# Four buffers for the split weights, tables that say how many are split ahead, and new orders of the units

## The chip, the core and the metric

The kernel runs on one core of one Trainium2 chip. Five engines work there side by side, each through its own list of instructions in order: TensorE (PE in the profile; PEld is its weight load), VectorE (DVE), ScalarE (ACT), GpSimd (POOL) and SyncE (SP), which here only issues DMAs. They wait for each other through semaphores. The metric is the device time of one execution in microseconds (us), the median of several runs; a profile is one execution with every instruction recorded.

## What is computed

Two transformer layers over 256 positions of width 2048, all in float32. Layer A: a norm, one projection to queries, keys, values and a forget gate, attention with 16 heads of 128, an output projection, a residual, then an MLP. Then keys and values for layer B are made once from the result, and layer B has its own queries, attention in chunks of 64, an output projection and an MLP. The MLP, on which this text turns, is

```python
def sq_relu_mlp(h, g, w1, w2):
    a = jax.nn.relu(rms_norm(h, g) @ w1)      # w1: 2048 x 8192
    return (a * a) @ w2                       # w2: 8192 x 2048
```

## The kernel before

**Three products per product.** A float32 weight is taken apart into two numbers that TensorE multiplies fast: `hi`, which ScalarE makes by copying the weight to the type fp32r, and `lo`, which VectorE makes as weight minus `hi`. The activations are held in the same way. `passes` then issues three rounds of matmuls: hi times hi (L592), hi times the activations' lo (L594), lo times hi (L596). The part of the weight that is split at a time is called a unit: 128 partitions by 1024 columns. It costs one ScalarE copy (L292), one VectorE subtraction (L293), and 12 matmuls of 512 columns when it is a plain unit.

**Seven products for eight.** In the MLPs and the query projection, a *pair* (two output panels `a` and `b`, both for both halves of the positions) does part of its depth by seven products of sums in place of eight products. The seven *forms* f0 to f6 are the weight block 11, then T3, T2, T1, 21, T4, 22: `FORMS = ("11", "T3", "T2", "T1", "21", "T4", "22")`. Each form has two units, each with only 6 matmuls. The sums of weight blocks are made on the way: T3 and T1 by a DMA that GpSimd issues and that adds as it writes (`add_on`, L324), T2 by VectorE (`make`, L331), T4 by VectorE (`add_on`, L322). The rest of the depth is 4 plain units for panel a (a4 to a7) and 4 for panel b (b4 to b7). The forms accumulate in four PSUM tiles, and three of these have to be combined on the way (the end of `form_products`): after f0 ScalarE writes `c`, after f1 it copies `P7`, after f2 VectorE makes `P7 - c` (L637) and after f3 `c - P7` (L639). f3 accumulates in the tile of `c`, and panel a's plain units in the tile that L637 writes, so both have to wait for L637. The names of the PSUM tiles alternate with the pair: `acc` in two of four, `s` and `po` in the others.

**The order.** A chunk of the MLP is four pairs: w10 and w11 (first weight matrix), w20 and w21 (second). Each layer has four chunks; layer A ends with the query pairs q0 and q1. `ORDER` holds a string per pair with the place of every unit: `f2` is both units of a form, `a` and `b` are this pair's next plain unit, `r` is a plain unit left over from the pair before (where none is left, it is passed over). `plan_mlp` turns it into one list, and the main loop takes it item by item: `fetch` (which splits units ahead), the matmuls, then `run_fill`, which issues the steps of finished panels that are due. When a panel's last unit is done, its results go off: `w1` panels are transposed by VectorE (L441) into a tile `z`, moved by 16 small DMAs into a tile `q` (L456, half of them issued by SP, half by GpSimd), then ScalarE applies relu (L954), squares it into `hi` (L959) and in float32 (L961), and VectorE takes the difference (L965). `HIDDEN`, `LONG`, `SHORT` and `QUERY` say after how many units each of these steps is issued. `BEHIND` says after which form the next sums of weights are issued. The order on TensorE, VectorE, ScalarE and SP is the written one; the instructions of GpSimd are placed by the scheduler.

**How far ahead.** `fetch` keeps three units split: the one about to be multiplied and two more (`AHEAD = 2`). `hi` and `lo` have three buffers each, so the fourth `hi` waits until TensorE has finished with the first. Copy and subtraction of a unit are issued together:

```python
def fetch(ahead=AHEAD, early=EARLY):
    while (units or raws) and len(ready) <= ahead:
        issue()                     # hi by ScalarE, lo by VectorE
```

The raw weights of forms f4, f6 and of the plain units come into three buffers of 128 x 2048 (`wraw`, two units each) by DMAs of 1 MB that SP issues (L279). `wsp = pool("wsp", 3)` in the listing is the pool of `hi` and `lo`.

Of the kernel before, what the change touches and what calls it, by code (L numbers as in the profile page):

```python
# [28 lines left out]
AHEAD = 2  # L29
EARLY = 4  # L30
HIDDEN = (
# [4 lines left out]
)  # L36
UA = UN // 512
LONG = (
# [4 lines left out]
)  # L43
SHORT = (
# [4 lines left out]
)  # L49
REL = 384  # L50
QUERY = (0, 1, 15, 10, 5, 17, 5)
AGAIN = (0, 1, 2, 3, 5, 5, 7, 7)
ATT = ((8, 14, 18, 18, 10), (8, 8, 12, 12, 9))
BIAS = (3, 6, 7)
ORDER = {
# [9 lines left out]
}  # L65
BEHIND = {
    (0, 0): [(2, 1, "add", "T1", 0), (0, 1, "make", 0)],
    (0, 1): [(0, 1, "make", 1)],
# [4 lines left out]
}  # L73
SUBS = {"1": (2, 2), "2": (2, 2), "q": (2, 2)}
OPENING = (
    (23, "bring", "12", 0),
    (19, "bring", "12", 1),
    (6, "add", "T3", 0),
    (9, "add", "T3", 1),
    (3, "bring", "11", 0),  # L80
    (4, "bring", "11", 1),
)
# [16 lines left out]
def trunk(ctx: ExitStack, tc: tile.TileContext, t):  # L99
# [8 lines left out]
    PSUM = bass.MemoryType.PSUM  # L108
    wsp = pool("wsp", 3)
    acts = pool("acts", 8)  # L110
# [37 lines left out]
    gqk = const.tile([P, 2], F32, name="gqk")  # L148
    flipper = const.tile([P, P], F32, name="flipper")
    V.tensor_copy(flipper, ident[:, ::-1])  # L150

# [21 lines left out]
    class Pair:  # L173

        def __init__(self, big, src, stage, n, subs):
            self.big, self.stage, self.n, self.subs = big, stage, n, subs
# [27 lines left out]
    def plan_mlp(layer, query, tail):  # L204
# [7 lines left out]
        for i, p in enumerate(pairs):  # L212
            own = [i for q in "ab" for u in p.plain for i in p.items(f"{q}{u}")]
            for j in ORDER["first" if not i else p.stage[0] + str(p.n) + ("+" if p.stage == ("w2", NCH - 1) else "")].split():
# [33 lines left out]
    n_out = 4 * KT // UA - 4  # L248
    units.extend(halves_of((w_in[i] for i in range(w_in.shape[0])), False))
    tail_a = Tail(stage_units(w_oa, 4))  # L250
# [30 lines left out]

    def issue():
        if not raws:
            load()
        item, raw, cuts, _ = raws.popleft()
        if not cuts:
            assert (FORMS[item.u], item.s) in item.pair.done
            raw, cuts = item.pair.t[FORMS[item.u]][:, half(item.s)], [slice(0, UN)]
        hi = wsp.tile([P, UN], F32R, name="hi")
        lo = wsp.tile([P, UN], F32R, name="lo")  # L290
        for c in cuts:
            S.activation(hi[:, c], raw[:, c], AF.Copy)  # L292
            V.tensor_tensor(lo[:, c], raw[:, c], hi[:, c].bitcast(F32), op=ALU.subtract)  # L293
# [41 lines left out]
    def behind(p, i, s):  # L335
        for k in range(s, 2 if s == p.subs - 1 else s + 1):
            for d, own, f, *a in BEHIND.get((i, k), ()):
# [199 lines left out]
    class RowStats:  # L537
# [39 lines left out]
        def flip(self):  # L577
            pm = ps_o.tile([P, 512], F32, name="pt", tag="po")
            TE.matmul(pm[:, :NB], flipper, self.ms, start=True, stop=True)
            f = RowStats(self.name + "f")  # L580
# [348 lines left out]
    rooms.open()  # L929
    for g in range(NG):  # L930
        zq, lq = turned("z")
# [17 lines left out]
    def mlp(plan, x, Sx, st, last, query=None):  # L949
# [49 lines left out]
        for it in plan:  # L999
            p, hl = it.pair, fetch()  # L1000
            assert it.u < 4 or it.kind == "f" or it.u * 2 < len(p.x or range(99)), (p.stage, p.n, it.u, len(p.x))
# [9 lines left out]
            if it.kind != "f" or it.s == p.subs - 1:  # L1011
                run_fill()
                q = {"f4": 0, "f5": 0, "f6": 1}.get(f"f{it.u}") if it.kind == "f" else it.kind
                if q is not None:
                    p.left[q] -= 1
                    if not p.left[q]:
                        for b in range(NB):
                            p.evac[q](b, p.ps[q][b])

    st1, x1, S1 = RowStats("m"), [], []  # L1020
    stage(o, [next_x(n, None, st1, 1, x1, fs=S1, then=st1.inverse if n == NG - 1 else None) for n in range(NG)], tail=tail_a, plan=plan_a)
    st2, xb, kept = RowStats("b"), [], []
    xkv, Sq, qs = [], [], []

    def query(g):
        box = {}

        def f(b, ps):
            if b == 0:
                z, lq = turned(), landing(2 + g % 2)  # L1030
                box["lq"], box["f"] = lq, head_norm(lambda: st2, z, lq, apart=(*QUERY[:2], None, None)[g])
            box["f"](b, ps)
            if b == NB - 1:
                add_fill([[]] * QUERY[2 + g] + [[lambda: qs.append(scale_q(box["lq"], 1, g))]])
                if g == 1:
# [5 lines left out]
    mlp(plan_a, x1, S1, st1, lambda n, r2: next_x(n, r2, st2, 3, xb, kept, Sq, st2.both if n == NG - 1 else None), (xb, Sq, query))  # L1041
    st2f = st2.flipped

    def rel_bias(g, box):
# [9 lines left out]

    o = [None] * H
    rooms.open()
    for g in range(NG):
# [85 lines left out]
```

## Time and profile before

| | |
|---|---|
| three runs | 2113.25, 2117.59, 2120.19 us; median 2117.59 |
| the profiled execution | 2115.48 us; span of its instructions 2113.7 us |
| mean granted clock of TensorE in it | 0.998 |
| busy: PE, PEld, DVE, ACT, POOL | 2074.7, 1695.1, 1736.8, 1301.9, 354.1 us |
| DMA | 538.89 MB, mean 255 GB/s |
| MLP of layer A, queries, MLP of layer B | about 370 to 1060, 1060 to 1150 and 1425 to 2110 us of the span |

In rows of the time line, the columns are the start and the length in us, engine, source line, operation, tile written and tiles read, and how many equal instructions follow each other; in brackets is the idle time of the engine before it and what ended it. The length of one matmul there is that of its whole way through the array. The next one enters long before, so distances from start to start tell the rate. In rows of waits come the total in us, the number and the longest. In rows of windows come, for each engine, the busy us and the count of instructions, then TensorE's granted clock, the busy share of the DMA engines and GB/s.

### The profile page before, as it was taken

What the parts mean: (1) busy time and instruction counts of PE and PEld (TensorE: products, weight loads), DVE (VectorE), ACT (ScalarE), POOL (GpSimd) and SP (SyncE); (2) the same over time, 40 slices, a digit from 0 to 9 for tenths busy, and PEclk for the clock granted to TensorE, in tenths of its full rate; (3) what the DMA queues carried; (4) which work ended last, traced back from release to release, by engine and by line L of the source; (5) the groups of instructions that cost most, each with busy time, mean ns of one, the idle gap of its engine ahead of it and who ended that gap; (6) DMA issues with size and microseconds to landing.
All of it is one profiled execution on the core that took longest, in us unless ns stands there. A gap on an engine that the chain in (4) does not pass through costs nothing.

```text
span 2113.7 us, 27078 instructions
## 1 busy us (share of the span) xinstructions
PE 2074.7 (98%) x9114; PEld 1695.1 (80%) x9114; DVE 1736.8 (82%) x2003; ACT 1301.9 (62%) x1567; POOL 354.1 (17%) x552
## 2 busy tenths in 40 slices
PE   9999999999999999999999999999999999999999
PEld 7888888787887887887777888887878878878877
DVE  6777776998889889878989577768988998898897
ACT  6544445676567567557767445456765765675674
POOL 1101002221031022022224000022200310220220
PEclk9999999999999999999999999999999999999999
DMA  8777788889888888898786777888897898888884
GB/s 302 241 257 222 240 253 266 251 257 283 273 256 245 277 267 244 262 278 268 239 241 218 256 235 241 239 265 251 268 278 256 259 259 279 268 250 256 280 262 157
DMA packets 160636, 538.89 MB, mean 255 GB/s; under 512 B 42849, under 2 KB 68081, under 8 KB 125681
## 3 DMA queue, kind: packets, MB, share of 16 engines
q1 hardware_dynamic: 129136, 453.78, 61.3%
q0 software_dynamic: 31360, 83.39, 20.8%
q8 instruction: 71, 1.16, 0.2%
q14 instruction: 69, 0.56, 0.1%
HBM read 497.20 MB, written 15.75 MB: 243 GB/s over the span
## 4 chain that ended last, share of the span: by engine, by line
PE 83%; DMA 6%; DVE 6%; issue 3%; ACT 2%; SPq 0%; POOL 0%; ACTq 0%; DVEq 0%; POOLq 0%
PE acc L592 18%; PE acc L594 18%; PE acc L596 18%; PE po L592 5%; PE po L596 5%; PE po L594 5%; PE s L596 4%; PE s L592 4%; PE s L594 4%; DVE lo L293 3%; DMA raw<-in_s2a 2%; DMA q<-z 2%; ACT hi L292 2%; DVE wT L322 1%; DMA raw<-in_s2b 1%
## 5 line engine op out<-in xcount | busy, mean ns | idle before, releaser
L293 DVE TENSOR_TENSOR lo<-raw,hi 128x1024 fp32r<-128x1024 f32 (+1 forms) x634 | 759.5, 1214 | 221.2 <-ACT hi L292 208.9
L292 ACT ACTIVATE hi<-raw 128x1024 fp32r<-128x1024 f32 (+1 forms) x634 | 660.4, 1054 | 386.7 <-PE acc L594 224.5
L592 PE MATMUL acc<-hi,act 128*128 128x512 f32 x1644 | 459.0, 394 | 9.9 <-DVE acc L637 4.4
L596 PE MATMUL acc<-lo,act 128*128 128x512 f32 x1644 | 449.1, 390 | 0.3 <-DVE lo L293 0.3
L594 PE MATMUL acc<-hi,act 128*128 128x512 f32 x1644 | 449.1, 390 | 0.0
L592 PEld LDWEIGHTS acc<-hi,act 128*128 128x128 f32 x1644 | 306.1, 188 | 79.5 <-DVE acc L637 7.9
L596 PEld LDWEIGHTS acc<-lo,act 128*128 128x128 f32 x1644 | 307.5, 188 | 66.8 <-DVE lo L293 2.4
L594 PEld LDWEIGHTS acc<-hi,act 128*128 128x128 f32 x1644 | 308.5, 188 | 65.5 <-DVE act L387 0.5
L292 ACT ACTIVATE hi<-w 128x1024 fp32r<-128x1024 f32 x204 | 215.1, 1056 | 100.6 <-PE acc L594 39.6
L293 DVE TENSOR_TENSOR lo<-w,hi 128x1024 fp32r<-128x1024 f32 x204 | 244.5, 1216 | 27.9 <-ACT hi L292 27.2
L456 POOL DMA_DIRECT2D q<-z x336 | 174.1, 608 | 464.1 <-DVE z L441 253.8
L292 ACT ACTIVATE hi<-wT 128x1024 fp32r<-128x1024 f32 x136 | 142.4, 1057 | 65.7 <-PE acc L594 27.0
L293 DVE TENSOR_TENSOR lo<-wT,hi 128x1024 fp32r<-128x1024 f32 x136 | 162.7, 1218 | 21.9 <-ACT hi L292 21.8
L596 PE MATMUL s<-lo,act 128*128 128x512 f32 x476 | 137.7, 394 | 2.6 <-DVE lo L293 2.4
L592 PE MATMUL s<-hi,act 128*128 128x512 f32 x476 | 136.4, 391 | 0.8 <-ACT hi L292 0.8
L594 PE MATMUL s<-hi,act 128*128 128x512 f32 x476 | 135.5, 389 | 0.0
L596 PEld LDWEIGHTS s<-lo,act 128*128 128x128 f32 x476 | 87.9, 188 | 27.0 <-DVE lo L293 9.7
L592 PEld LDWEIGHTS s<-hi,act 128*128 128x128 f32 x476 | 89.4, 188 | 20.6 <-ACT hi L292 2.0
L594 PEld LDWEIGHTS s<-hi,act 128*128 128x128 f32 x476 | 89.5, 188 | 18.8
L691 POOL TENSOR_TENSOR rn<-vv,mhalf 128x4 f32<-128x4 f32 x32 | 44.3, 1398 | 336.4 <-DVE vv L690 336.3
L331 DVE TENSOR_TENSOR wT<-w,w 128x1024 f32<-128x1024 f32 x68 | 82.7, 1217 | 0.0
L322 DVE TENSOR_TENSOR wT<-wT,raw 128x1024 f32<-128x1024 f32 x68 | 82.7, 1216 | 0.0
(183 smaller groups left out, 2282.1 us busy)
## 6 DMA issues: line engine op xcount, KB each, us to landing
raw<-in_w_in SPq DMA_DIRECT2D x94, 512.0 KB, 5.5
raw<-in_s1a SPq DMA_DIRECT2D x32, 1024.0 KB, 6.4
raw<-in_s2a SPq DMA_DIRECT2D x32, 1024.0 KB, 6.9
raw<-in_w_kv SPq DMA_DIRECT2D x64, 512.0 KB, 5.5
raw<-in_s1b SPq DMA_DIRECT2D x32, 1024.0 KB, 7.0
raw<-in_s2b SPq DMA_DIRECT2D x32, 1024.0 KB, 6.7
raw<-in_w_oa SPq DMA_DIRECT2D x32, 512.0 KB, 6.3
w<-in_f1a SPq DMA_DIRECT2D x16, 1024.0 KB, 7.0
```

Of the source, the lines that this page charges most:

```text
L292: S.activation(hi[:, c], raw[:, c], AF.Copy)
L293: V.tensor_tensor(lo[:, c], raw[:, c], hi[:, c].bitcast(F32), op=ALU.subtract)
L322: V.tensor_tensor(d, d, p.t["21", s], op=ALU.add)
L331: V.tensor_tensor(p.t["T2"][:, half(s)], p.t["T3"][:, half(s)], p.t["11"][:, half(s)], op=ALU.add)
L456: (SY, G)[j % 2].dma_start(d[32 * j : 32 * j + 32, i], z[32 * i : 32 * i + 32, j * n : (j + 1) * n])
L592: TE.matmul(ps, xh, cut(hi, j), start=first, stop=False, **kw)
L594: TE.matmul(ps, xl, cut(hi, j), start=False, stop=False, **kw)
L596: TE.matmul(ps, xh, cut(lo, j), start=False, stop=last, **kw)
L691: G.tensor_tensor(rn, vv, mhalf, op=ALU.pow)
```

## The change

No arithmetic is added or removed: per engine the two programs issue the same operations, save that a copy of a mirrored identity (`flipper`) moves from the start of the kernel to the place of its only use.

- `hi` and `lo` get four buffers in place of three. Room for this comes from `flipper`, which now has a passing tile, and from the scratch space of GpSimd's DMAs, 2048 bytes a partition in place of 8192.
- `issue` is cut in two: `high` (ScalarE's copy) and `low` (VectorE's subtraction). `fetch` takes two numbers. `LOOK` says, by pair and form, how many units are wholly split ahead (2 before, now 1 to 3), and `MORE` how many more get their `hi` alone (0 to 2); at most four are open.
- `ORDER`, `HIDDEN`, `LONG`, `SHORT`, `QUERY` and the opening are dealt out anew, and `BEHIND` now has a table for each kind of pair.
- The scaled queries are kept by number, with checks of their order. `MINI` (off) builds the first MLP alone.

```diff
-    (1, 3, 3, 3, 6, 8, 8, 9, 11, 11),
+    (2, 3, 3, 5, 8, 8, 9, 10, 11, 12),
...
+LOOK = {
+    "w10": (2, 1, 2, 2, 3, 1, 2, 2),
...
+MORE = {
+    "w10": (1, 2, 0, 0, 0, 0, 0, 0),
...
-    "w11": "f0 r f1 r f2 f4 a r f3 r a a f5 a f6 b b",
-    "w20": "r f0 r r f1 f2 f4 f3 f5 a r r a r b f6 b",
-    "w21": "f0 f1 f2 r f3 f4 r a f5 r r f6 r b a r",
+    "w11": "f0 f1 r f2 r r f4 a f3 r a a r r f5 a f6 b b",
+    "w20": "r f0 r f1 f2 f4 r f3 f5 a r a f6 b r r",
+    "w21": "f0 f1 f2 r r f3 r f4 r r r r a f6 f5 r a b r",
...
-    wsp = pool("wsp", 3)
+    wsp = pool("wsp", AHEAD + 2)
...
-    def issue():
+    highs = deque()
+
+    def high():
         if not raws:
             load()
         item, raw, cuts, _ = raws.popleft()
...
         hi = wsp.tile([P, UN], F32R, name="hi")
+        for c in cuts:
+            S.activation(hi[:, c], raw[:, c], AF.Copy)
+        highs.append((item, raw, cuts, hi))
+
+    def low():
+        if not highs:
+            high()
+        item, raw, cuts, hi = highs.popleft()
         lo = wsp.tile([P, UN], F32R, name="lo")
         for c in cuts:
-            S.activation(hi[:, c], raw[:, c], AF.Copy)
             V.tensor_tensor(lo[:, c], raw[:, c], hi[:, c].bitcast(F32), op=ALU.subtract)
...
-    def fetch(ahead=AHEAD, early=EARLY):
-        while (units or raws) and len(ready) <= ahead:
-            issue()
+    def fetch(ahead=AHEAD, early=EARLY, more=0):
+        while (units or raws or highs) and len(ready) <= ahead:
+            low()
+        while (units or raws) and len(ready) + len(highs) <= ahead + more and can_high():
+            high()
...
-            p, hl = it.pair, fetch()
+            p = it.pair
+            if isinstance(p, Pair):
+                n = it.u if it.kind == "f" else 7
+                hl = fetch(LOOK[p.key][n], more=MORE[p.key][n])
+            else:
+                hl = fetch()
...
-    nc = bacc.Bacc("TRN2", target_bir_lowering=False, num_devices=1, dynamic_dma_scratch_size=8192)
+    nc = bacc.Bacc("TRN2", target_bir_lowering=False, num_devices=1, dynamic_dma_scratch_size=2048)
```

Three places show what the tables do. In all of them the names are those of the second chunk of layer A (the numbers are the program's own). `wT2` is the tile that holds T2 and later T4, `raw` is a block of raw weights.

VectorE, before, at form f4 of pair w11 (`raw_5002` is its block, `po_4718` and `po_4719` are panel b of w10, whose last unit b7 stands between f1 and f2 on TensorE; L322 makes T4):

```order
L441 STREAM_TRANSPOSE z_5172<-po_4718 128x4x4x32
L441 STREAM_TRANSPOSE z_5172<-po_4719 128x4x4x32
L293 TENSOR_TENSOR lo_5177<-raw_5002,hi_5176 128x1024
L322 TENSOR_TENSOR wT2_5040<-wT2_5040,raw_5002 128x1024
L293 TENSOR_TENSOR lo_5190<-raw_5002,hi_5189 128x1024
L322 TENSOR_TENSOR wT2_5040<-wT2_5040,raw_5002 128x1024
L637 TENSOR_TENSOR acc_5083<-p7_5153,acc_5084 128x512
L293 TENSOR_TENSOR lo_5209<-raw_5080,hi_5208 128x1024
```

The same engine and place in the change, where `raw_4978` is b7 of w10 (now between f2 and f4 on TensorE), `raw_4990` the block of f4, and L673 the former L637:

```order
L319 TENSOR_TENSOR lo_5151<-raw_4978,hi_5149 128x1024
L319 TENSOR_TENSOR lo_5164<-raw_4990,hi_5154 128x1024
L348 TENSOR_TENSOR wT2_5034<-wT2_5034,raw_4990 128x1024
L673 TENSOR_TENSOR acc_5076<-p7_5119,acc_5077 128x512
L319 TENSOR_TENSOR lo_5176<-raw_4990,hi_5167 128x1024
L348 TENSOR_TENSOR wT2_5034<-wT2_5034,raw_4990 128x1024
L475 STREAM_TRANSPOSE z_5195<-po_4719 128x4x4x32
L475 STREAM_TRANSPOSE z_5195<-po_4720 128x4x4x32
L319 TENSOR_TENSOR lo_5201<-raw_5090,hi_5199 128x1024
```

The combination after f2 moved from behind both units of f4 to between them, and the transposes from the front to the end.

ScalarE, before, in pair w20 (`raw_5403` holds a4 and a5, `raw_5557` b4 and b5, `raw_5637` f6; L954 is the relu of panel b of w11, which reads the `q` that the small DMAs write):

```order
L292 ACTIVATE hi_5633<-raw_5403 128x1024
L292 ACTIVATE hi_5645<-raw_5403 128x1024
L954 ACTIVATE q_5524<-q_5524 128x1024
L292 ACTIVATE hi_5661<-raw_5557 128x1024
L292 ACTIVATE hi_5681<-raw_5637 128x1024
```

The same in the change (`raw_5540` is f6, `raw_5616` b4 and b5, `w11_5660` f0 of the next pair; the relu is now L990):

```order
L310 ACTIVATE hi_5614<-raw_5403 128x1024
L310 ACTIVATE hi_5638<-raw_5403 128x1024
L310 ACTIVATE hi_5656<-raw_5540 128x1024
L310 ACTIVATE hi_5677<-raw_5540 128x1024
L310 ACTIVATE hi_5694<-raw_5616 128x1024
L310 ACTIVATE hi_5698<-w11_5660 128x1024
L310 ACTIVATE hi_5712<-w11_5660 128x1024
L990 ACTIVATE q_5525<-q_5525 128x1024
```

The relu moved behind five copies, among them that for b4.

VectorE, before, in pair w21, from the second T4 to the first unit of f6 (`raw_5686` is f4's block, `raw_5667` a7 of w20, `raw_5813` a4, `raw_5853` b6 and b7 of w20, `raw_5888` f6; L728 adds a finished panel to the residual):

```order
L322 TENSOR_TENSOR wT2_5731<-wT2_5731,raw_5686 128x1024
L639 TENSOR_TENSOR acc_5765<-acc_5764,p7_5806 128x512
L293 TENSOR_TENSOR lo_5875<-raw_5667,hi_5874 128x1024
L293 TENSOR_TENSOR lo_5885<-raw_5813,hi_5884 128x1024
L293 TENSOR_TENSOR lo_5897<-wT2_5731,hi_5896 128x1024
L728 SCALAR_TENSOR_TENSOR h0_90<-s_5479,qm_3608,h0_90 128x512
L728 SCALAR_TENSOR_TENSOR h1_91<-s_5480,qm_3608,h1_91 128x512
L293 TENSOR_TENSOR lo_5917<-wT2_5731,hi_5916 128x1024
L293 TENSOR_TENSOR lo_5933<-raw_5853,hi_5932 128x1024
L293 TENSOR_TENSOR lo_5945<-raw_5853,hi_5944 128x1024
L293 TENSOR_TENSOR lo_5955<-raw_5888,hi_5954 128x1024
```

The same in the change (`raw_5700` is f4's block, `raw_5794` b6 and b7 of w20, `raw_5854` a4, `raw_5899` f6, which lies in the buffer that `raw_5700` had):

```order
L319 TENSOR_TENSOR lo_5862<-raw_5700,hi_5852 128x1024
L675 TENSOR_TENSOR acc_5748<-acc_5747,p7_5781 128x512
L319 TENSOR_TENSOR lo_5873<-raw_5700,hi_5864 128x1024
L348 TENSOR_TENSOR wT2_5710<-wT2_5710,raw_5700 128x1024 x2
L319 TENSOR_TENSOR lo_5897<-raw_5794,hi_5895 128x1024
L319 TENSOR_TENSOR lo_5909<-raw_5794,hi_5907 128x1024
L319 TENSOR_TENSOR lo_5915<-raw_5854,hi_5913 128x1024
L319 TENSOR_TENSOR lo_5933<-raw_5899,hi_5931 128x1024
```

Between T4 and f6 stand three subtractions now, and before nine instructions; f5 moved behind f6.

More of the change, by code (lines that the diff above doesn't have):

```diff
@@ L75 @@
 OPENING = (
[L76 to L81, printed above, removed]
+    (18, "bring", "12", 0),
+    (16, "bring", "12", 1),
+    (9, "add", "T3", 0),
+    (5, "add", "T3", 1),
+    (4, "bring", "11", 0),
+    (12, "bring", "11", 1),
 )
@@ L213, in plan_mlp @@
             own = [i for q in "ab" for u in p.plain for i in p.items(f"{q}{u}")]
-            for j in ORDER["first" if not i else p.stage[0] + str(p.n) + ("+" if p.stage == ("w2", NCH - 1) else "")].split():
+            for j in ORDER["first" if not i else p.key + ("+" if p.stage == ("w2", NCH - 1) else "")].split():
                 if j in "r":
@@ L248, in trunk @@
     n_out = 4 * KT // UA - 4
-    units.extend(halves_of((w_in[i] for i in range(w_in.shape[0])), False))
+    if not MINI:
+        units.extend(halves_of((w_in[i] for i in range(w_in.shape[0])), False))
     tail_a = Tail(stage_units(w_oa, 4))
@@ L336, in behind @@
         for k in range(s, 2 if s == p.subs - 1 else s + 1):
-            for d, own, f, *a in BEHIND.get((i, k), ()):
+            for d, own, f, *a in BEHIND[p.key].get((i, k), ()):
                 q = p if own else p.next
@@ L344, in trunk, with can_high @@
     WAYS = {"make": make, "add": add_on, "bring": bring}
-    def fetch(ahead=AHEAD, early=EARLY):
-        while (units or raws) and len(ready) <= ahead:
-            issue()
+    def can_high():
+        if not raws:
+            load()
+        item, _, cuts, _ = raws[0]
+        return cuts or (FORMS[item.u], item.s) in item.pair.done
+    def fetch(ahead=AHEAD, early=EARLY, more=0):
[3 more added lines that the diff above has]
+            high()
         while units and sum(r[3] for r in raws) < early:
@@ L578, in flip @@
             pm = ps_o.tile([P, 512], F32, name="pt", tag="po")
+            flipper = wk.tile([P, P], F32, name="flipper", tag="wk")
+            V.tensor_copy(flipper, ident[:, ::-1])
             TE.matmul(pm[:, :NB], flipper, self.ms, start=True, stop=True)
@@ L929, in trunk @@
     rooms.open()
-    for g in range(NG):
+    for g in range(0 if MINI else NG):
         zq, lq = turned("z")
@@ L1018, in mlp @@
                             p.evac[q](b, p.ps[q][b])
+    if MINI:
+        for i in range(H):
+            o[i] = quarter(i)
+            if i % GH == 0:
+                G.memset(part[0].bitcast(F32), 0.0)
     st1, x1, S1 = RowStats("m"), [], []
@@ L1022, in trunk, with scale, free @@
     st2, xb, kept = RowStats("b"), [], []
-    xkv, Sq, qs = [], [], []
+    xkv, Sq, qs = [], [], {}
+    def scale(g, lq):
+        assert g >= 2 or len(xkv) >= 2 * GH
+        qs[g] = scale_q(lq, 1, g)
+    def free(g):
+        assert g in qs
     def query(g):
@@ L1029, in f @@
             if b == 0:
+                if g >= 2:
+                    add_fill([[]] * 2 + [[lambda: free(g - 2)]])
                 z, lq = turned(), landing(2 + g % 2)
```

24 lines of the change are left out of this document (17 added, 7 removed), and 48 rows, old and new, of tables (BEHIND, HIDDEN, LONG, LOOK).

## The prediction

> **What bounds the kernel now.** I read the page's head first, then the stages in a view of windows, then TensorE's waits, then the time line at each kind of stop.
>
> ```profile
> span 2113.7 us, 27078 instructions
> PE 2074.7 (98%) x9114; PEld 1695.1 (80%) x9114; DVE 1736.8 (82%) x2003; ACT 1301.9 (62%) x1567; POOL 354.1 (17%) x552
> ...
> 655.77 1.07 PE L594 MATMUL s<-hi,act 128*128 128x512 f32 x4
> 656.68 1.09 PE L596 MATMUL s<-lo,act 128*128 128x512 f32 x4
> ```
>
> TensorE is the bound. Four matmuls take 656.68 − 655.77 = 0.91 us from start to start, 0.2275 us each. That rate shows what a stretch loses:
>
> ```profile
> 398.00:1060.00 662.00, 648.87 (x2822) 526.05 (x2821) 582.09 (x588) 438.40 (x471) 130.40 (x215) 1.00 0.86 262
> 1060.00:1155.00 95.00, 88.54 (x375) 71.83 (x374) 86.10 (x98) 67.77 (x90) 29.26 (x40) 0.96 0.76 231
> 1453.00:2109.50 656.50, 647.07 (x2818) 525.42 (x2816) 568.76 (x565) 423.47 (x439) 114.90 (x187) 1.00 0.84 258
> 1069.00:1081.00 12.00, 8.10 (x24) 6.16 (x23) 9.88 (x12) 8.43 (x14) 5.33 (x9) 0.72 0.98 262
> ```
>
> Layer A's MLP: 662.0 − 2822 × 0.2275 = 20.0 us lost. Queries: 95.0 − 375 × 0.2275 = 9.7. Layer B's MLP: 656.5 − 2818 × 0.2275 = 15.4. Together 45.1 us, 2% of the span: the change removes no matmul, so this is all that its tables can win in these stages. VectorE is 88% busy there (582.09 of 662), so it is locally the bound. The waits name the places:
>
> ```profile
> PE po L592 <- DVE s L637: 12.7, 9, 3.9
> PE acc L592 <- DVE acc L637: 4.4, 8, 0.6
> PE po L592 <- ACT hi L292: 3.6, 5, 1.1
> PE acc L592 <- ACT hi L292: 3.1, 4, 0.9
> PE s L596 <- DVE lo L293: 2.4, 8, 0.8
> ```
>
> Eight chunks explain the counts: `acc` L637 is a4 of w11, eight of the nine `s` L637 are f3 of w20 (the ninth, 3.9, is q0), and `hi` is mostly b4 of w20.
>
> **Part 1: a4 of w11.** TensorE and VectorE there, second chunk:
>
> ```profile
> 604.93 0.62 PE L592 MATMUL acc<-hi,act 128*128 128x512 f32 x2
> 606.10 0.73 PE L592 MATMUL acc<-hi,act 128*128 128x512 f32 x2 [0.55 <-DVE acc L637]
> 606.68 1.08 PE L594 MATMUL acc<-hi,act 128*128 128x512 f32 x4
> ...
> 599.62 1.31 DVE L441 STREAM_TRANSPOSE z<-po 128x512 f32<-128x512 f32 x2
> 600.85 1.18 DVE L293 TENSOR_TENSOR lo<-raw,hi 128x1024 fp32r<-128x1024 f32 x1
> 601.96 1.21 DVE L322 TENSOR_TENSOR wT<-wT,raw 128x1024 f32<-128x1024 f32 x1
> 603.09 1.22 DVE L293 TENSOR_TENSOR lo<-raw,hi 128x1024 fp32r<-128x1024 f32 x1
> 604.23 1.22 DVE L322 TENSOR_TENSOR wT<-wT,raw 128x1024 f32<-128x1024 f32 x1
> 605.37 0.68 DVE L637 TENSOR_TENSOR acc<-p,acc 128x512 f32<-128x512 f32 x1
> ```
>
> From 604.93 to 606.68 four matmuls take 1.75 us in place of 0.91: 0.84 lost. L637 needs only f2, but VectorE runs two transposes and both halves of f4 and T4 (5.75 us, 599.62 to 605.37) ahead of it. In the change b7 is multiplied between f2 and f4, and L673 stands behind one half of f4 and T4; the transposes, the other half and its T4 follow. Two of four instructions of 1.14 us leave its path, the transposes (1.23) too: 3.5 us earlier, against 0.84 needed, with b7's 12 × 0.2275 = 2.73 us of cover more. The stop goes: 8 × 0.84 = **−6.7** (ends −6.7 and 0). What is late next is the transposes' panel; b7 ends 2.73 later relative to f2, and its results are due in w20, units away.
>
> **Part 2: f3 of w20.**
>
> ```profile
> 638.73 0.62 PE L592 MATMUL po<-hi,Sh 128*128 128x512 f32 x2
> 649.16 0.70 PE L592 MATMUL po<-hi,Sh 128*128 128x512 f32 x2 [1.10 <-DVE s L637]
> ...
> 639.77 1.30 DVE L441 STREAM_TRANSPOSE z<-acc 128x512 f32<-128x512 f32 x2
> 641.40 2.36 DVE L293 TENSOR_TENSOR lo<-wT,hi 128x1024 fp32r<-128x1024 f32 x2 [0.32 <-ACT hi L292]
> 643.78 1.23 DVE L293 TENSOR_TENSOR lo<-raw,hi 128x1024 fp32r<-128x1024 f32 x1
> 648.33 0.69 DVE L637 TENSOR_TENSOR s<-p,po 128x512 f32<-128x512 f32 x1
> ```
>
> From f1's start to f3's are 36 matmuls, 8.19 us, that took 649.16 − 638.73 = 10.43: 2.24 lost, of which the row shows 1.10 as idle. VectorE works from 639.77 to 649.02 with one gap of 0.32: 8.93 us of work behind the end of w11's b7. That is more than TensorE's 8.19, and the change leaves all of it there: its order on VectorE still has transposes, f2, f4 and T4 ahead of the combination. What can go is the gap of 0.32, which waits for ScalarE (a fourth buffer and an earlier `hi` act on it), and the 639.77 − 638.73 = 1.04 by which VectorE starts late: I take 0.8 of these 1.36 for each of eight chunks, **−6.4** (ends −10.9, both whole, and 0). About 1.1 us a chunk remain, since VectorE's work is not less.
>
> **Part 3: b4 of w20.**
>
> ```profile
> 658.86 1.06 ACT L954 ACTIVATE q<-q 128x1024 f32<-128x1024 f32 x1 [4.55 <-DMA q<-z]
> ...
> 659.42 1.07 PE L596 MATMUL s<-lo,act 128*128 128x512 f32 x4
> 660.92 1.19 PE L592 MATMUL po<-hi,act 128*128 128x512 f32 x4 [0.43 <-ACT hi L292]
> ```
>
> ScalarE stands 4.55 us in front of the relu, for the small DMAs, with b4's `hi` queued behind; TensorE then waits for that `hi`. In the change five copies, b4's among them, come before the relu, so the DMAs' time is covered by splitting. The two rows of `hi` above sum to 3.6 + 3.1 = 6.7 us in nine stops; some are not b4's, so I take two thirds, **−4.5** (ends −6.7 and 0). What is late next is the relu, then the activations of panel b. Neither order has a6, a7, b6 or b7 of w20, which read them, before w21's first forms: they hide it as long as the moves land.
>
> **Part 4: the queries, f3 of q0.**
>
> ```profile
> 1069.16 0.61 PE L596 MATMUL po<-lo,S 128*128 128x512 f32 x2
> 1073.68 1.19 PE L592 MATMUL po<-hi,S 128*128 128x512 f32 x2 [3.90 <-DVE s L637]
> 1079.79 0.63 PE L594 MATMUL s<-hi,act 128*128 128x512 f32 x2
> ...
> 1071.70 1.23 DVE L293 TENSOR_TENSOR lo<-w,hi 128x1024 fp32r<-128x1024 f32 x1 [2.12 <-ACT hi L292]
> ...
> 1060.76 0.97 POOL L324 DMA_DIRECT2D w<-in_fqb  x1
> ...
> DMA to landing us min/median/max: 5.5/6.9/9.7
> ```
>
> The second half of T1 is issued by GpSimd at 1060.76, behind six moves, and lands 9.7 us later, the longest of these; ScalarE, VectorE and L637 follow, and TensorE stands 3.90 us. Then its clock drops, 0.72 in the window 1069 to 1081: 14 matmuls from 1073.68 to 1079.79 take 6.11 in place of 3.19, 2.9 more. The change keeps f2 and f3 adjacent and the same six moves ahead of T1. Ends: −5.7 (a landing at 6.9 saves 2.8 of the wait and the clock's 2.9) and +1 (f3's wait grows with a later queue). I take **−2.0**, nearer to no change because its cause is not touched. [...]
>
> **Part 5: what the change adds.** The orders place f6 of w21 sooner after f4. f6's raw block takes f4's buffer, free only after the second T4. Between them TensorE has b6, b7 and a4, 36 × 0.2275 = 8.19 us; before it had a7, a4, f5, b6 and b7, 60 × 0.2275 = 13.65. Less ScalarE's copy (1.06) and VectorE's subtraction, which works beside the first matmuls, a load has some 7.2 us.
>
> ```profile
> DMA to landing us min/median/max: 3.7/6.2/12.1
> ...
> q0 software_dynamic: 31360, 83.39, 20.8%
> ```
>
> The raw loads take 6.2 in the middle, 12.1 at most. A load at the median costs nothing, one at 12.1 about 4.9. Over eight chunks I take half of them 0.6 late: **+2.5** (ends 0 and 8 × 4.1 = 33, all loads at 11.3). The smaller scratch space of GpSimd's DMAs, the moved `flipper` and the two functions of `fetch` add no instruction; I cost them at nothing. The first names a risk: 31360 packets go through GpSimd's queue. [...]
>
> **The sum.** −6.7 − 6.4 − 4.5 − 2.0 + 2.5 = −17.1. The profiled execution took 2115.5 us (span 2113.7 and 1.8 around it), 2.1 below the median of the runs: 2115.5 − 17.1 = 2098.4, or 2100.5 against the median of 2117.6. I say **2100**.
>
> **Rivals.**
>
> *VectorE stays the bound.* For it: 88% busy in the MLPs, and f3's 8.93 us of work against 8.19. Then only the order in w11 pays, and of b4 a part: −6.7 − 2.3 + 2.5 = −6.5, 2111. Against it: w20 shows gaps that a fourth buffer closes.
>
> *All stops but the forced ones go.* 45.1 less f3's remaining 8 × 1.1 = 8.8 and about 7 at the first pair, the queries and stage starts: −29, 2089. For it: VectorE has 80 us free in each MLP. Against it: q0's cause stays.
>
> *Slower: raw blocks late at f6 of w21.* The place is part 5's. It cancels the rest when loads pass about 7.2 + 19.6/8 = 9.7 us there, and at 11.3 costs 33: 2117.6 − 19.6 + 33 = 2131; at 10.6, 27 and 2125. For it: a maximum of 12.1, and 86% busy DMA engines that faster stages would load more. Against it: the median of 6.2.
>
> *Slower: GpSimd's moves queue.*
>
> ```profile
> q<-z POOLq DMA_DIRECT2D x336, 32.0 KB, 6.1
> ```
>
> If the smaller scratch makes each of its DMAs wait for the one before, a move costs its landing, 6.1 us, in place of its issue, and eight in a row 49 us, more than a pair hides: 0.25 us late in each of 32 pairs is 8 us and 2125. For or against it no row speaks.
>
> *The tables do nothing.* The same instructions are issued, and VectorE and TensorE keep their work: 2117.6.
>
> **How the numbers follow.** Chances: the forecast 0.55, VectorE the bound 0.15, all stops 0.08, raw blocks late 0.14, moves queue 0.04, nothing 0.04. A change of 0.3%, 6.4 us, is about what a measurement of this kernel can tell from none; faster ends at 2111.2, slower begins at 2123.9. Faster: 0.55 + 0.08 + 0.08, half of the second, = 0.71. The same: 0.07 + 0.04 = 0.11. Slower: 0.18. The range begins at 2084 (parts 1 to 3 at their ends, −24.3, q0 at its end, −5.7, which is 2087.6, and 3.6 of the other stops) and reaches to 2119, past the case of nothing: left out is what is slower, 0.18. The forecast's own range is 2090 to 2109.
>
> **What will show it.** Right: in TensorE's waits the row for L673 at `acc` is gone; f3 of w20 keeps a stop, near 0.5 of idle; `hi` no longer stops b4; q0's f3 still waits, and the clock dips there; the MLP windows hold 20.0 and 15.4 us less about 9 each. Wrong: a new row in which `hi` waits for the raw loads and TensorE for `hi` at f6 of w21; moves that take over 6 us on GpSimd; or f3 of w20 with 1.10 of idle as before, which would say that VectorE's work alone sets it.

## The result

| | median us | lowest to highest | against the kernel before |
|---|---|---|---|
| before, 20 runs | 2118.05 | 2113.04 to 2126.24 | |
| changed, 20 runs | 2111.01 | 2105.50 to 2116.84 | 0.9966 (0.9955 to 0.9976) |

The change is 7.0 us faster, 0.34%. The direction was forecast, and the time lies in the range (2084 to 2119), but 17 us were forecast and less than half of them came. The profiled execution of the changed kernel took 2111.67 us, 0.7 above its median, that of before 2115.48, 2.6 below its own; so the two traces differ by only 3.8 us of the 7.0. The ratios in this text leave out one execution of run 6, which took 8183 us.

The granted clock may hold a part of the rest. It was 0.9987 on average in the 20 executions of the changed kernel, and 0.9974 in 65 executions of the kernel before that were taken later, beside the experiments; from these two and the span an estimate is 0.0013 × 2114 = 2.7 us. That the clock makes this part of the difference is not shown. In the two traces the granted clock stood at 0.50 for 6.8 us, before in one stretch from 1073.0, in the change in two of 3.4 from 1068.5 and 1147.0.

First the head of the page, the windows of the two MLPs and the queries, and TensorE's waits, all of the changed kernel:

```profile
span 2109.9 us, 26958 instructions
...
PE 2073.8 (98%) x9114; PEld 1698.1 (80%) x9114; DVE 1722.0 (82%) x2003; ACT 1292.4 (61%) x1567; POOL 354.8 (17%) x552
```

```profile
398.00:1060.00 662.00, 652.07 (x2845) 531.41 (x2844) 583.01 (x593) 439.51 (x476) 134.07 (x220) 1.00 0.87 264
1060.00:1155.00 95.00, 88.66 (x376) 71.86 (x375) 86.70 (x102) 66.83 (x89) 28.37 (x37) 0.96 0.74 233
1453.00:2109.50 656.50, 644.10 (x2810) 524.97 (x2808) 562.61 (x564) 420.94 (x442) 115.12 (x186) 1.00 0.84 257
```

```profile
PE po L628 <- DVE s L673: 11.5, 11, 3.0
PE acc L632 <- DVE lo L319: 7.3, 13, 0.8
PE acc L628 <- ACT hi L310: 5.0, 11, 1.7
```

In the first window 2845 matmuls ran, 23 more than before in the same 662 us. The row of the accumulator that waits for `P7 - c` is gone from the waits; the row of `acc` in which the lo-pass (the third round of matmuls, with `lo`) waits for VectorE's subtraction has 13 entries, and before it had 2 (0.7 us). Where the time went is best seen by unit. The table sums, over all chunks, by how much each matmul of the weights starts later than 0.229 us after the one before it (excesses under 0.03 left out), put down to the unit of the later one. In the rows of the projections and of keys and values this holds attention's own matmuls too, which are the same in both:

| lost by starts, us | before | changed | forecast of the difference |
|---|---|---|---|
| w11, nearly all at a4 | 7.1 | 0 | −6.7 |
| w20, f1 to f3 | 17.2 | 9.2 | −6.4 |
| w20, b4 | 4.1 | 0 | −4.5 |
| w20, f0 | 2.2 | 0 | none |
| w20, a6 to b7, taken in w21 | 1.2 | 1.3 | none |
| w21 | 4.0 | 17.2 | +2.5 |
| q0 | 8.2 | 6.5 | −2.0 |
| q1 | 0.2 | 1.3 | none |
| w10 and the units ahead of it | 5.5 | 7.1 | none |
| keys and values | 16.8 | 20.2 | none |
| the projections | 35.9 | 36.2 | none |
| together | 102.5 | 99.0 | −17.1 |

By layers, the MLP of layer A loses 17.1 us in place of 22.5, that of layer B 17.7 in place of 18.7. The stops that the forecast removed are removed, with some more: w11 and w20 together lose 21.3 us less (31.8 to 10.5), for 17.6 forecast. They are paid back in w21 above all, 13.2 us, and there at its start. There the rows of SP, ScalarE, VectorE and TensorE in the second chunk read:

```profile
646.44 4.06 SPq L490 DMA_DIRECT2D q<-z  x6
650.67 0.46 SPq L337 DMA_DIRECT2D w<-in_f2a  x1
```

```profile
661.58 2.01 ACT L310 ACTIVATE hi<-w 128x1024 fp32r<-128x1024 f32 x2 [6.06 <-DMA w<-in_f2a]
...
670.64 0.60 ACT L671 ACTIVATE p<-acc 128x512 f32<-128x512 f32 x1 [0.70 <-PE acc L632]
671.13 1.05 ACT L310 ACTIVATE hi<-wT 128x1024 fp32r<-128x1024 f32 x1
```

```profile
646.50 2.36 DVE L319 TENSOR_TENSOR lo<-w,hi 128x1024 fp32r<-128x1024 f32 x2
...
662.67 1.23 DVE L319 TENSOR_TENSOR lo<-w,hi 128x1024 fp32r<-128x1024 f32 x1 [4.13 <-ACT hi L310]
663.81 1.22 DVE L357 TENSOR_TENSOR wT<-w,w 128x1024 f32<-128x1024 f32 x1
664.95 1.22 DVE L319 TENSOR_TENSOR lo<-w,hi 128x1024 fp32r<-128x1024 f32 x1
666.08 1.22 DVE L357 TENSOR_TENSOR wT<-w,w 128x1024 f32<-128x1024 f32 x1
667.22 2.35 DVE L319 TENSOR_TENSOR lo<-w,hi 128x1024 fp32r<-128x1024 f32 x2
```

```profile
666.22 0.73 PE L632 MATMUL acc<-lo,act 128*128 128x512 f32 x2 [0.42 <-DVE lo L319]
...
668.49 0.73 PE L632 MATMUL acc<-lo,Sh 128*128 128x512 f32 x2 [0.62 <-DVE lo L319]
...
672.24 0.72 PE L628 MATMUL acc<-hi,Sh 128*128 128x512 f32 x2 [0.28 <-ACT hi L310]
```

The load of w21's block 11 (`w<-in_f2a`) is issued at 650.67 and is there at 661.5, 10.8 us later. ScalarE stands 6.06 us for it, and VectorE idles 4.13 with nothing to do. Then four subtractions and two sums for T2 have to be made in a row while TensorE runs f0 and f1 at 1.37 us a unit: stops at f0/1 and f1/0. The third stop, at f2/1, has another cause: the copy for it (671.13) stands behind the copy of P7 (670.64), which waits for f1's own matmuls. Before, b5 stood between f6 and f0 and gave the load 2.73 us more.

### The profile page after: what moved, and what is told of

It reads as the page before. It is cut to its first block, busy times and chain, and to the rows that moved or that the text cites. A ratio compares the mean times of both kernels' runs of the same rounds, so it can differ in the third digit from the quotient of the medians.

```text
span 2109.9 us, 26958 instructions
## 1 busy us (share of the span) xinstructions
PE 2073.8 (98%) x9114; PEld 1698.1 (80%) x9114; DVE 1722.0 (82%) x2003; ACT 1292.4 (61%) x1567; POOL 354.8 (17%) x552
## 4 chain that ended last, share of the span: by engine, by line
PE 73%; DMA 10%; DVE 9%; issue 4%; ACT 3%; SPq 1%; DVEq 0%; ACTq 0%; POOL 0%; POOLq 0%
PE acc L628 16%; PE acc L632 16%; PE acc L630 16%; DVE lo L319 6%; PE po L628 4%; PE po L632 4%; PE po L630 4%; PE s L632 3%; PE s L630 3%; PE s L628 3%; DMA w<-in_f2b 2%; DMA w<-in_f2a 2%; ACT hi L310 2%; DMA q<-z 1%; SPq L490 1%
## 5 line engine op out<-in xcount | busy, mean ns | idle before, releaser
L310 ACT ACTIVATE hi<-w 128x1024 fp32r<-128x1024 f32 x204 | 210.8, 1054 | 110.6 <-PE po L630 30.3
L319 DVE TENSOR_TENSOR lo<-wT,hi 128x1024 fp32r<-128x1024 f32 x136 | 161.3, 1218 | 17.7 <-ACT hi L310 17.2
L630 PEld LDWEIGHTS s<-hi,act 128*128 128x128 f32 x476 | 89.2, 188 | 20.2 <-DVE act L1001 1.6
L350 POOL DMA_DIRECT2D w<-in_f1a x32 | 28.6, 967 | 324.6 <-ACT hi L310 113.2
```

The lines of the kernel that those rows point to most:

```text
L350: G.dma_start(d, p.big[block][:, half(s)], accum_op=ALU.add)
L630: TE.matmul(ps, xl, cut(hi, j), start=False, stop=False, **kw)
```

## The experiments

The names of the lines are those of each kernel (some lines up or down where an edit adds or takes lines).

**1. The order of w11 alone, in the kernel before.**

```diff
-    "w11": "f0 r f1 r f2 f4 a r f3 r a a f5 a f6 b b",
+    "w11": "f0 f1 r f2 r r f4 a f3 r a a r r f5 a f6 b b",
```

> The kernel before with one line of its order table exchanged, that of pair w11 (b7 of w10 between f2 and f4, and so on as in the change). The forecast's part 1: the eight stops of a4 of w11 on L637 (4.4 us of idle, 6.7 us by starts) go, the ratio to before is about 0.997 (2111), and f3 of w20 keeps its stops. Rival, that VectorE stays the bound and the stop only moves on: the row of a4 goes, but as much comes back within w11 or at f3 of w20, ratio 0.999 to 1.001.

Measured: 2136.26 us, ratio 1.0071 (1.0048 to 1.0093). Neither theory. The stop at a4 is gone, in all eight chunks; but b7 of w11, which is multiplied behind f0 of w20 as before, lost 19.8 us, and b4 of w20 9.0 in place of 4.1. ScalarE, and TensorE at one of these b7:

```profile
638.05 1.30 ACT L405 ACTIVATE Sh<-sum 128x512 fp32r<-128x512 f32 x2 [4.50 <-DVE sum L400]
639.26 1.04 ACT L292 ACTIVATE hi<-raw 128x1024 fp32r<-128x1024 f32 x1
...
640.35 1.19 PE L592 MATMUL acc<-hi,act 128*128 128x512 f32 x4 [1.55 <-ACT hi L292]
```

ScalarE's step on the sums (L405) stands 4.50 us for VectorE, and the copy for b7 stands behind it. How many units after a panel's end these steps come is said by another table, HIDDEN, and that had not moved.

**2. The order of w11 and the step table, in the kernel before.** The edit of 1, and HIDDEN as in the change:

```diff
 HIDDEN = (
-    (1, 3, 3, 3, 6, 8, 8, 9, 11, 11),
-    (0, 2, 2, 2, 7, 8, 8, 8, 10, 10),
-    (1, 1, 1, 5, 5, 5, 9, 9),
-    (1, 1, 3, 4, 4, 6, 8, 10),
+    (2, 3, 3, 5, 8, 8, 9, 10, 11, 12),
+    (0, 2, 3, 3, 6, 7, 7, 7, 9, 9),
+    (1, 1, 2, 3, 5, 5, 8, 9),
+    (0, 3, 4, 4, 7, 8, 9, 10),
 )
```

> The kernel before with w11's order of the change, as in the first run of this study, and with the table HIDDEN of the change beside it, which says how many units after a panel's end its steps are issued. That first run took a4's stop away and lost 20 us at b7 of w11, where copies stood behind a step that waited for VectorE's sums. If the old step table did that, these 20 us go and the ratio to before is 0.996 to 0.999. If the order itself needs copies further ahead (the tables LOOK and MORE), the stops at b7 stay, ratio 1.004 to 1.008.

Measured: 2113.59 us, ratio 0.9972 (0.9959 to 0.9985). The old step table did it: w11 loses 0.3 us now. By the time, part 1 is worth what it was said to be, but only with the table that belongs to it. By starts the stop moved on: b4 of w20 loses nothing any more (4.1 before), but f0/1 of w20 9.1 (2.2 before), again behind the same step, and in all this trace loses only 0.7 us less than that of before. What the other 5 us of the medians are is not shown.

**3. Four buffers alone, in the kernel before.** `hi` and `lo` with four buffers, the smaller scratch space and the moved `flipper` that pay for it; no table, no order.

```diff
-    wsp = pool("wsp", 3)
+    wsp = pool("wsp", 4)
...
-    flipper = const.tile([P, P], F32, name="flipper")
-    V.tensor_copy(flipper, ident[:, ::-1])
...
+            flipper = wk.tile([P, P], F32, name="flipper", tag="wk")
+            V.tensor_copy(flipper, ident[:, ::-1])
...
-dynamic_dma_scratch_size=8192
+dynamic_dma_scratch_size=2048
```

> The kernel before with four buffers for hi and lo, paid for as in the change (scratch space of GpSimd's DMAs 2048 in place of 8192, flipper in a passing tile); two units ahead as before, no tables, all orders as before. If earlier copies close VectorE's gaps (part 2's reading), f3 and f4 of w20 lose some of their 20 us and the ratio is 0.996 to 0.998. If depth without the tables does nothing, since fetch never opens a fourth unit but only finds the buffer free sooner, the ratio is 0.999 to 1.001. If the smaller scratch space makes GpSimd's DMAs wait (the fourth rival), moves that take more than 0.5 us on GpSimd show, and the ratio is above 1.002.

Measured: 2112.80 us, ratio 0.9969 (0.9954 to 0.9983): by itself as much as the whole change. TensorE's waits:

```profile
PE po L592 <- DVE s L637: 13.9, 11, 2.7
PE po L592 <- ACT hi L290: 5.1, 7, 1.4
PE acc L592 <- DVE acc L637: 4.4, 8, 0.6
```

The stops of parts 1 and 2 are all there (4.4 as before, f3 11.9 by starts as before). What went is elsewhere and was not forecast: q0 loses 5.0 in place of 8.2 and f0 of w20 0.3 in place of 2.2; b4 of w20 rose from 4.1 to 5.8. Over the trace that is 2.9 us, of the 7.8 that the medians differ. Its executions had a granted clock of 0.9985 on average, those of before beside them 0.9973, some 2.6 us by the same estimate; the rest is not accounted for. In the trace of the change, which has the same smaller scratch, GpSimd's moves take 0.50 us each at the median, as before: it costs nothing that can be seen.

**4. The change without LOOK and MORE.**

```diff
+LOOK = {k: (2,) * 8 for k in ("w10", "w11", "w20", "w21", "q0", "q1")}
+MORE = {k: (0,) * 8 for k in ("w10", "w11", "w20", "w21", "q0", "q1")}
```

> The changed kernel with LOOK 2 and MORE 0 everywhere: new orders and four buffers, but as many units split ahead as before. If the tables carry what was won at w20 (stops of f0, f4, f3 and b4: 24.7 us before, 10.5 now), at least 5 us of it come back and the ratio to before is 0.999 to 1.001. If the orders alone carry it, the ratio stays at 0.9955 to 0.9975.

Measured: 2168.69 us, ratio 1.0217 (1.0192 to 1.0243), far more than the tables had been thought to carry.

**5. The change with MORE 0 and LOOK as it is.**

> The changed kernel with MORE 0 everywhere and LOOK as in the change: no copy of ScalarE runs ahead of its subtraction. The kernel without both tables lost 49 us, at units whose copy stands behind a waiting ScalarE step (Sh behind VectorE's sums). If copies ahead of those steps are what MORE is for, most of it, 30 us or more, is lost here too: ratio 1.010 to 1.020. If LOOK carries it, the ratio stays below 1.000.

Measured: 2171.28 us, ratio 1.0241 (1.0222 to 1.0259): without MORE, LOOK gains nothing, so MORE carries it. (LOOK at 2 beside MORE as it is was not run.) A row of ScalarE's waits in the change, and the same row without MORE:

```profile
ACT Sh L439 <- DVE sum L434: 24.7, 16, 2.8
```

```profile
ACT Sh L432 <- DVE sum L427: 63.9, 16, 4.5
```

Sixteen times ScalarE stands for VectorE's sums, 4.0 us each without the copies ahead, 1.5 with them (3.0 in the kernel before). It does not matter that ScalarE is only 61% busy in the change: each copy behind the step is late by that much, and the losses stand where the first unit behind it is (f0/1 of w20 10.8, b4 of w11 8.7, f1/1 of w10 10.0, f3 of w20 17.2 by starts). The new orders are about 50 us worse than the old without the copies ahead, and 7 better with them.

**6. The load of block 11 earlier in SP's queue.**

```diff
-    "w20": ... (3, 1): [(5, 0, "bring", "11", 0), (2, 0, "bring", "11", 1)] ...
+    "w20": ... (3, 1): [(1, 0, "bring", "11", 0), (1, 0, "bring", "11", 1)] ...
```

> The changed kernel with one row of BEHIND for w20 altered: the load of block 11 for w21 is issued by SP one unit behind f3 in place of five, so ahead of a raw block and six small moves in SP's queue. Theory of the late block: in the change this load is issued at 650.67, lands 10.8 us later, ScalarE stands 6.06 us for it, and the units f0 to f2 of w21 follow each other too fast for VectorE to catch up. Then about 10 of the 15 us of new stops at f0, f1 and f2 of w21 (eight chunks) go, and the ratio to before is about 0.992 (2100 to 2102). Rival theory, that VectorE simply has too much work there since b5 of w20 no longer stands ahead of f0: the load is earlier, the stops of 0.6 to 0.9 at f1 and f2 stay, and the ratio is 0.996 to 0.997.

Measured: 2125.94 us, ratio 1.0025 (1.0009 to 1.0040): slower than before, which neither theory had. VectorE at f3 of w20, SP, then ScalarE:

```profile
648.20 2.35 DVE L319 TENSOR_TENSOR lo<-w,hi 128x1024 fp32r<-128x1024 f32 x2
```

```profile
650.57 0.33 SPq L337 DMA_DIRECT2D w<-in_f2a  x1
650.96 0.44 SPq L295 DMA_DIRECT2D raw<-in_s2a  x1
```

```profile
664.38 1.06 ACT L310 ACTIVATE hi<-raw 128x1024 fp32r<-128x1024 f32 x1 [9.44 <-DMA raw<-in_s2a]
```

The load uses T1's tile, which the subtractions of f3 read until 648.20 + 2.35 = 650.55 here, and it goes out at 650.57. In the change they are done at 646.50 + 2.36 = 648.86 and the load goes at 650.67, so its place in the queue can give 1.8 us at most. And while SP waits at the head of its queue, a raw block and six moves stand behind it: the block, issued at 646 in the change, now comes too late, and b4 of w20 loses 13.1 us by starts. Whether the load's lateness makes the stops was left open by this run; an earlier place in SP's queue does not mend it.

**7. Block 11 in two loads.**

```diff
+            for h in [slice(0, UN), slice(UN, 2 * UN)] if name == "11" and p.key == "w21" else [slice(0, p.subs * UN)]:
-            SY.dma_start(p.t[name][:, : p.subs * UN], p.big[name])
+                SY.dma_start(p.t[name][:, h], p.big[name][:, h])
```

> The changed kernel with block 11 of w21 loaded by two DMAs of 512 KB in place of one of 1 MB, at the same place in SP's queue. Theory of the late block: ScalarE's wait of 6 us for it, at f0 of w21, shrinks by 2 us or more, and with it the stops behind it, 4 to 10 of 16 us; ratio to before 0.992 to 0.995. Rival, VectorE's work alone: ScalarE's wait shrinks, the stops at f1 and f2 stay, ratio 0.996 to 0.997. If both halves land when the whole did, nothing moves.

Measured: 2105.89 us, ratio 0.9933 (0.9915 to 0.9952). f0 needs only the first half, which is there sooner. ScalarE's wait for the load in layer B, in the kernel before, in the change, and with two loads:

```profile
ACT hi L292 <- DMA w<-in_f2b: 1.3, 1, 1.3
```

```profile
ACT hi L310 <- DMA w<-in_f2b: 18.5, 4, 6.5
```

```profile
ACT hi L310 <- DMA w<-in_f2b: 13.9, 6, 4.1
```

In layer A the longest went from 6.1 to 5.1. These 1.0 and 2.4 us are enough: f0/1 of w21 loses 0 (2.5 in the change), f1/0 1.2 (6.7); f2/1 keeps its 5.3, which hangs on P7's copy. VectorE has the same work there in both, so it was the late load that made the stops at f0 and f1.

**8. b5 of w20 put back ahead of w21.**

```diff
-    "w20": "r f0 r f1 f2 f4 r f3 f5 a r a f6 b r r",
+    "w20": "r f0 r f1 f2 f4 r f3 f5 a r a f6 b b r r",
```

> The changed kernel with b5 of w20 put back ahead of f0 of w21 (as before the change), 12 matmuls or 2.73 us more of TensorE's work ahead of f0. The stops at f0, f1, f2 of w21 and the a6 behind them sum to 16 us by starts in the change and to nothing before it. If removing b5 caused them, at least 10 us of them go; the ratio to before is then 0.990 to 0.994, unless the step tables, which count units, now fit worse (the first run of this study lost 20 us at b7 of w11 that way), in which case a new row of hi behind a waiting ScalarE step stands in their place and the ratio is 0.997 or more.

Measured: 2112.07 us, ratio 0.9963 (0.9949 to 0.9976), the same as the change. f0 and f1 lose 1.4 us (9.5 in the change): that b5 was taken away caused those stops. But f6 of w21 loses 8.7 in place of 2.2 and f3 of w20 10.9 in place of 9.2, and a row of ScalarE's waits that held 6.7 us in the change reads

```profile
ACT hi L310 <- DMA raw<-in_f2b: 20.1, 3, 6.7
```

It is the rival on the raw blocks of f6, at its place and with its mechanism: the plain unit that stood between f4 and f6 is now ahead of f0. The time is the same at either place of the unit.

**9. T2 of w21 made by GpSimd.**

```diff
-        V.tensor_tensor(p.t["T2"][:, half(s)], ...)
+        (G if p.key == "w21" else V).tensor_tensor(p.t["T2"][:, half(s)], ...)
```

> The changed kernel with T2 of w21 made by GpSimd in place of VectorE, two additions of 128x1024 that take 1.22 us each on VectorE and stand between the first three subtractions of w21. Rival theory, VectorE has too much work there: the stops at f1/0 (6.7 us by starts over eight chunks) and f0/1 (2.5) go, f2 may stop instead for GpSimd's slower addition; ratio 0.993 to 0.996. If the late block alone decides, f1/0 keeps 0.8 a chunk. If GpSimd's addition is several times VectorE's 1.22 us, f2 waits for it and the kernel is slower than the change.

Measured: 2123.28 us, ratio 1.0008 (0.9994 to 1.0021), slower than the change. f1/0 loses nothing any more, but f0/1 15.6 in place of 2.5 and f0/0 5.2 in place of 0.3. GpSimd and VectorE there:

```profile
665.91 5.74 POOL L357 TENSOR_TENSOR wT<-w,w 128x1024 f32<-128x1024 f32 x2 [13.46 <-DMA w<-in_f2a]
```

```profile
666.94 8.06 DVE L319 TENSOR_TENSOR lo<-w,hi 128x1024 fp32r<-128x1024 f32 x4 [4.13 <-ACT hi L310]
```

Four subtractions take 8.06 us here, and 4.63 in a row of the change where GpSimd does nothing (at 1161.16). TensorE waits for the first two:

```profile
669.46 0.73 PE L632 MATMUL acc<-lo,act 128*128 128x512 f32 x2 [0.75 <-DVE lo L319]
...
672.79 0.73 PE L632 MATMUL acc<-lo,act 128*128 128x512 f32 x2 [1.68 <-DVE lo L319]
```

So the first took about 2.5 us from 666.94 and the second about 3.3, and the other two 2.2 together, to 675.00; GpSimd's additions end at 671.65. The run cannot tell what VectorE's work costs there: VectorE did not get faster by giving work away.

**10. Two units ahead at f1 of w21.**

```diff
-    "w21": (2, 1, 2, 2, 1, 2, 2, 2),
+    "w21": (2, 2, 2, 2, 1, 2, 2, 2),
```

> The changed kernel with one number of LOOK altered: at f1 of w21 two units are split ahead in place of one, so the copy for the second half of T2 stands ahead of ScalarE's copy of P7 (L671) in place of behind it. Expected: the 5.3 us of stops at f2/1 of w21 (0.88 each in six chunks) go, ratio to before 0.994 to 0.996. Rival, VectorE's work: it has no slack there, the subtraction comes no earlier than now, and the stop stays or moves to the units behind, ratio 0.9965.

Measured: 2109.39 us, ratio 0.9961 (0.9948 to 0.9974). The stops at f2/1 go, all 5.3 us, and f1/0 keeps 6.3; but a6 behind them rises from 1.3 to 3.6 and others by as much. The time cannot be told from the change's.

**11. The scaled queries later.**

```diff
-QUERY = (0, 1, 14, 10, 3, 15, 3)
+QUERY = (0, 1, 14, 10, 5, 17, 3)
```

> The changed kernel with two numbers of QUERY as they were before (the scaled queries of the third and fourth group two units later). In the change ScalarE stands 10.27 us for a small DMA ahead of one of these scalings, at the start of keys and values, with copies of weights behind it, and TensorE loses 2.0 us at the fifth unit. Expected: that stop goes, the kernel is 2 us faster than the change, 0.995 to 0.9965 to before; otherwise the wait is only moved and nothing changes.

Measured: 2112.43 us, ratio 0.9957 (0.9937 to 0.9977). In the change ScalarE, and behind it TensorE, read

```profile
1159.03 1.15 ACT L754 ACTIVATE q<-land,gqk 128x1024 f32<-128x1024 f32 x1 [10.27 <-DMA land<-turn]
...
1161.18 1.20 PE L628 MATMUL acc<-hi,act 128*128 128x512 f32 x4 [1.72 <-ACT hi L310]
```

and with the later scalings

```profile
1162.17 1.15 ACT L754 ACTIVATE q<-land,gqk 128x1024 f32<-128x1024 f32 x1 [3.50 <-DMA land<-turn]
```

with no stop of TensorE behind it. The 2.0 us there go in the trace; the time alone is too uncertain to show them.

**12. Three of these together:** two loads, two units ahead at f1 of w21, the later scalings.

> The changed kernel with three edits together: block 11 of w21 in two loads, the scaled queries of the third and fourth group two units later, and two units ahead at f1 of w21. If the three stops are independent, their sum goes: 9 to 11 us at f0 and f1, 5 at f2, 2 at keys and values; ratio to before 0.989 to 0.992 (2096 to 2102). If they share one bound, VectorE's work at w21, the ratio stays at 0.993, that of the two loads alone.

Measured: 2104.21 us, ratio 0.9928 (0.9913 to 0.9943), the lowest median of the study, by the two ratios 0.4% faster than the change. Its waits:

```profile
PE po L629 <- DVE s L674: 12.6, 11, 3.0
PE acc L629 <- ACT hi L310: 4.1, 6, 1.4
PE acc L633 <- DVE lo L319: 3.5, 6, 0.8
```

By starts 89.6 us are lost, 9.4 fewer than in the change: f0 to f2 of w21 0.9 in place of 14.8, keys and values 16.8 as before the change. f6 and a6 take 5 back. It cannot be told from two loads alone (0.9933), though the traces differ by 4.7 us. What remains largest in the MLPs, f3 of w20 with 10.3, waits for VectorE.

## Why the prediction was right and wrong

**The bound** was right: TensorE, whose stops are all that can be won. The stops did shrink by as much as the traces' spans differ, 3.5 of 3.8 us.

**Part 1** was right in size: 7.1 us went for 6.7 forecast. What it left out is that w11's order needs the step table beside it: without it the same edit costs 15 us (run 1), with it the time falls as forecast (run 2), though by starts a stop at f0/1 of w20 comes in the place of the one at a4; the change has neither.

**Part 2** was right in its mechanism and a little small: f1 to f3 of w20 lost 8.0 less, 6.4 forecast. VectorE starts 0.1 us behind TensorE's f1 (637.77) in place of 1.04 and is busy without a gap from 637.89 until L673, so both of the shares that the forecast took in part went almost whole in this chunk. f3 keeps 0.65 of idle, and by starts 9.2 us over eight chunks, 1.15 each. The prediction's own sum leaves 2.24 − 0.8 = 1.44 a chunk, not the 1.1 that it names. The fourth buffer, which it credits with the gap, does not close it alone (run 3: f3 as before); without MORE f3 loses 17.2 us (run 5). The stop that is left:

```profile
646.74 0.70 PE L628 MATMUL po<-hi,Sh 128*128 128x512 f32 x2 [0.65 <-DVE s L673]
```

**Part 3** was right: 4.1 went for 4.5. In run 2 the step table and w11's order take this stop away without any of the rest; with the order alone it grew to 9.0 (run 1).

**Part 4** was right in size, 1.7 for 2.0, for another reason. Four buffers alone took 3.2 us there (run 3), with ScalarE still 2.6 us in front of T1 and 2.7 of idle on TensorE. In the change ScalarE waits only 0.26 us for T1; VectorE, busy without a gap, has two transposes and two subtractions ahead of L673, and its work sets the stop of 3.00 us:

```profile
1063.49 1.06 ACT L310 ACTIVATE hi<-w 128x1024 fp32r<-128x1024 f32 x1 [0.26 <-DMA w<-in_fqb]
```

```profile
1067.36 0.70 PE L628 MATMUL po<-hi,S 128*128 128x512 f32 x2 [3.00 <-DVE s L673]
```

The forecast's end of −5.7 counts the clock's 2.9 us as saved with 2.8 less of idle. In the change the idle is 0.9 less, and the granted clock still fell to 0.50, for 3.4 us in place of 6.8; with 2.98 of idle it did not fall in run 10. A window of 18 us in the change, and in run 10:

```profile
1060.00:1078.00 18.00, 15.00 (x60) 11.91 (x59) 16.97 (x18) 11.45 (x17) 5.85 (x10) 0.91 0.95 282
```

```profile
1060.00:1078.00 18.00, 15.02 (x66) 11.99 (x65) 16.46 (x17) 11.34 (x17) 5.80 (x10) 1.00 0.95 279
```

In runs 7 and 12 the idle there was 2.99, and two matmuls behind it took 0.85 us from start to start; in run 10 they took 0.46. In the change the clock fell to 0.50 a second time, at the first unit of keys, behind stops of 0.86 and 1.66 us; the trace of before has stops of 0.90 and 1.66 there, and a granted clock of 1.00. So the length of one stop does not tell. In the change four matmuls take 1.71 us there in place of 0.91:

```profile
1148.27 1.91 PE L630 MATMUL acc<-hi,act 128*128 128x512 f32 x4
1149.98 1.30 PE L632 MATMUL acc<-lo,act 128*128 128x512 f32 x4
```

**Part 5 is the step that failed**, by its size and its place. It gave +2.5 us to new waits and looked for them at f6 of w21; those came to about 1 us. Parts 1 to 4 together brought what they were to bring, 20.9 us for 19.6. But 14.8 us came at f0 to f2 of w21, where nothing was lost before and which the prediction put at nothing: it read the order of VectorE behind f4 there, but not that taking b5 away left the load of block 11 without cover. Of these, two loads returned 8.2 us by starts (run 7) and two units ahead at f1 the 5.3 at f2/1 (run 10). Another 2.0 us of QUERY's two numbers were not priced at all, and 1.4 us at the first unit of keys are matmuls at the granted clock of 0.50 shown above, which was not priced either.

**Rivals.** That raw blocks come late at f6 was the wrong place in the change, though run 8 shows it is only one plain unit away. That VectorE stays the bound gave 2111, the measured time, but by luck, not by its mechanism: w20 paid in full. That all stops but the forced ones go failed at the same start of w21. GpSimd's moves did not queue: 0.50 us each at the median in both traces. And the buffers, which the sum priced at a few tenths in f3 of w20, give 0.31% alone (run 3), with none of the gains of parts 1 to 3. In the trace their gains stand at q0 (3.2 us) and f0 of w20 (1.9), where the change gains 1.7 and 2.2; so a part of what the tables seem to win there may be the buffers'. Whether the gains of buffers and tables add up was not shown: the change's tables ask for the fourth buffer, and no run has them without it.

## What to carry over

Where an engine issues in written order, a table that moves work has to be read with every step that waits on that engine: the copy behind a waiting step is late by the whole wait, 4.0 us each in run 5, even on an engine that is busy only 61% of the change's span. Before a unit is taken from between two others, look for the transfer that was running beside it, and from when its buffer is free; the load that waited for its buffer gained nothing by an earlier place in its queue (run 6, issued at 650.57 for 650.67), but in two parts it let the first use start sooner (run 7, a longest wait of 4.1 us for 6.5 in layer B). A saving in a list of stops is worth what the next stop leaves of it, so price the units that come closer together, not only those that the wait moves away from.

## What was not expected of the hardware

VectorE was slower while GpSimd added: four subtractions of VectorE took 8.06 us beside two additions of GpSimd of 2.9 us each (run 9), and 4.63 with GpSimd doing nothing (the change, at 1161.16), 3.4 less. What made them slower was not shown, and what GpSimd's additions take with VectorE idle was not measured.
